# Nine instead of eight up tiles in seven half products, in a new order, and another step into the MLP

## The chip, the cores and the metric

The kernel runs on one core of a Trainium2 chip. PE (TensorE) multiplies; DVE (VectorE), ACT (ScalarE) and POOL (GpSimd) work element by element; SP only issues DMA transfers, and POOL issues some too. The metric is the device time of one execution in microseconds; where several runs are shown, their median.

## The reference

One layer of an encoder trunk over 512 tokens of width 1024, in float32: an RMS norm, one input projection, three groups of attention heads, an output projection into the residual; then the part that the change touches, the gated MLP with a causal convolution of width 3, followed by a gated per-layer input.

```python
def conv_gated_mlp(h, w_up, conv_w, conv_b, w_down):
    u = h @ w_up
    S = u.shape[1]
    up = jnp.pad(u, ((0, 0), (CONV_WIDTH - 1, 0), (0, 0)))
    c = conv_b
    for j in range(CONV_WIDTH):
        c = c + conv_w[j] * up[:, j:j + S]
    gate, val = jnp.split(c, 2, axis=-1)
    return (jax.nn.silu(gate) * val) @ w_down
...
        h = h + conv_gated_mlp(rms_norm(h, ln_ffn[i]), w_up[i], conv_w[i], conv_b[i], w_down[i])
        gate = jax.nn.sigmoid(rms_norm(h, ln_ple[i]) @ w_ple_gate[i])
        h = h + (p[i] @ w_ple_proj[i]) * gate
```

`w_up` is 1024 x 5632, `w_down` 2816 x 1024.

## The kernel before, in words

Every float32 operand of a product is split into a high part (`hi`, fp32r, a cast on ACT) and a low part (`lo`, the difference, on DVE), and a product is three matmuls: hi x hi, hi x lo and lo x hi. Weights come in by DMA on SP's queue into a ring of 7 raw tiles, and their splits go into a ring of 7 pairs (`NRAW`, `NHI`). So a split waits for a landed load and for a free pair, and a load for a raw tile whose split is done.

The attention stage runs first, in slots. Its PE order is written out; the order on ACT and DVE is the scheduler's. In its slots 20 to 45 SP also copies sums' first terms from DRAM to DRAM (`COPIES`, `copy_sum`), dealt out evenly over what `_sums` lists: four copies for every tile of `SEVEN`, and four for each of four groups of down weights.

The step into the MLP is written out by hand (from `add_sums()` to the last `ple_unit`), and its order on PE, ACT, DVE, POOL and SP is kept. The last output products (`last_out`) and the squares of the residual run; a matmul with ones (`total`) adds the squares over partitions into `pst`; `roots` makes the inverse root (a logarithm and an exponential on ACT, four operations on DVE) into `rb2`; `norm(k)` makes row block k of the normed residual `hn` and casts it to `Th`, `low(k)` gives `Tl`. Meanwhile PE multiplies the per-layer input: `ple_product(j)` makes the eight products `pp` of six matmuls each, `ple_keep(j)` copies one out of PSUM on ACT (`pps`) and stores it by SP; `ple_unit(j)` is both. `first_split(f, i)` splits piece i of the weights of up tile f, for the first two tiles.

The MLP has 22 up tiles of 128 gate and 128 value columns. The first two are done together, row block by row block, as `Th` comes. Each of the others goes one of two ways:

- plain (`up_plain`, letter P, three pieces): gate and value columns, 8 row blocks, three matmuls each, 48 matmuls of 512 tokens; weights of 768 + 768 + 512 columns.
- in seven half products (`up_seven`, letter S, six pieces): gate and value as a 2 x 2 block product over even and odd row blocks and two halves of the tokens, by a scheme of Strassen's kind with 7 products instead of 8. 84 matmuls of 256 tokens; weights of four times 768 and once 512 columns, of which the last 2048 come from `usum`, sums of weight blocks in DRAM. These sums are made by transfers that add (`add_sums`, issued by POOL, two in flight, four for each S tile and eight for each down group) on top of the copies. ACT copies results out of PSUM and DVE adds them (`su`) before the convolution.

Either way a chain follows (`ff_chain`: start on ACT, two taps on DVE for each of gate and value, SiLU, product), and for each pair of tiles the left operands of the down products (`left`). The down products (`Down`, letter D) use the same seven-product scheme, in groups of up tiles 0-5, 6-11, 12-17 and 18-21.

`ORDER` gives the order of these pieces on PE: it is kept as written. `tiles_of(ORDER)` numbers the tiles 2 to 21 as their first pieces come, so the letters also say which tiles are S. Everything else in the MLP (loads, splits, copies, chains, additions) is set in order by the planner at the end of the kernel: it gives each task a due time from the PE order and its list of estimated costs, then takes at each step, among tasks that could start about now, the one due first. The engines then keep that order.

Of the kernel before, what the change touches and what calls it, by code (L numbers as in the profile page):

```python
# [45 lines left out]
PHASES = (0, 6, 12, 18, 22)  # L46


ORDER = ("PPPPSSSSSPPSPPSSSSPSPPSPPDDDDDDDSPSSSSDSDDDPDDDSSSSSPSPPSSSSSPSPSSSDSSDDDSDPDDDDDDDDDPPPSSSSSPPSPSSSPSSPSPPPPPPP")


def tiles_of(order):

    f, n, tiles = 2, {"P": 0, "S": 0}, {"P": [], "S": []}
    for c in order:
        if c in n:
            if n[c] == 0:
                tiles[c].append(f)
                f += 1
            n[c] = (n[c] + 1) % {"P": 3, "S": 6}[c]  # L60
    assert f == NF and not any(n.values()), (f, n)
    return tiles["P"], tiles["S"]


PLAIN, SEVEN = tiles_of(ORDER)

# [11 lines left out]
def kernel(ctx: ExitStack, tc: tile.TileContext, x, xt0, xt, pt_in, small, bias_c,  # L78
# [35 lines left out]
    def bank(tag, name):  # L114
        return ps.tile([P, 512], F32, tag=tag, bufs={"z": 2, "s": 2, "t": 3, "o": 1}[tag], name=name)
# [122 lines left out]
    def mm3(acc, ah, al, bh, bl, first, last, **k):  # L238
        pe.matmul(acc, ah, bh, start=first, stop=False, **k)
        pe.matmul(acc, ah, bl, start=False, stop=False, **k)  # L240
        pe.matmul(acc, al, bh, start=False, stop=last, **k)
# [675 lines left out]
    def mtmp(dt, m, name):  # L917
        return mp.tile([P, S * m], dt, tag="conv", bufs=CONV, name=name)
# [8 lines left out]
    def total(tag, sums):  # L927

        pst = bank(tag, "pst")
        pe.matmul(pst, onec.broadcast_to([P, P]), sums, start=True, stop=True)  # L930
        return pst

    def roots(pst, rb, mt, sq):

        act.activation(rb, pst, AF.Ln, scale=1.0 / D, bias=epsc)
        dve.tensor_scalar(mt, pst, 1.0 / D, EPS, ALU.mult, ALU.add)
        act.activation(rb, rb, AF.Exp, scale=-0.5)
        dve.tensor_tensor(out=sq, in0=rb, in1=rb, op=ALU.mult)
        dve.scalar_tensor_tensor(sq, sq, -0.5, mt, ALU.mult, ALU.mult)
        dve.scalar_tensor_tensor(rb, sq, 1.5, rb, ALU.add, ALU.mult)  # L940
# [20 lines left out]
    def ple_product(j):  # L961
        PP[j] = acc = bank("tttzsttt"[j], f"pp_{j}")
        for k in range(2):
            a, b = (w[:, j % 4 * P : (j % 4 + 1) * P] for w in WPP[j // 4, k])
            mm3(acc, a, b, *pT[k], k == 0, k == 1)

    def ple_keep(j):
        pp = mtmp(F32, 1, f"pps_{j}")
        act.copy(pp, PP[j])
        sp.dma_start(out=pp_d[j], in_=pp)  # L970

    def ple_unit(j):
        ple_product(j)
        ple_keep(j)
# [279 lines left out]
    def up_plain(f):  # L1254

        ws, w, more = plain_weights(f)
        us = Slot("z"), Slot("s")

        def some(g, ks):
            def do():  # L1260
                c = g * NF + f
                if ks[0] == 0:
                    U[c] = bank("zs"[g], f"u{c}")
                for k in ks:
                    mm3(U[c], *w(g, k), Th[k // 4][:, k % 4, :], Tl[k // 4][:, k % 4, :], k == 0, k == KD - 1)
            return do

        for g in range(2):
            pe_task(36, some(g, range(6)), [more()], (), [us[g]])
            yield  # L1270
        last = []
        more()
        for g in range(2):
            last.append([pe_task(12, some(g, range(6, KD)), [ws[2]], (), (), [us[g]])])
        ff_chain(f, None, last, ((us[0],), (us[1],)))
        yield
# [131 lines left out]
    def first_split(f, i, later=False):  # L1408
        w = first_w[f][0][i]
        lows = [] if later else None  # L1410
        w.hi, w.lo = split(w.t, w.n, lows=lows)
        w.split.end = 0.0
        return lows[0] if later else None

    def two_adds():
        for q in [q for q in EARLY_ADDS if q.end is None][:2]:
            q.do()
            q.end = 0.0
# [22 lines left out]
        last_sq = sq  # L1441
    todo[7]()
    two_adds()
    for j in range(3):
        ple_unit(j)
    first_split(1, 0)
    ple_unit(3)
    rb2, work = (mp.tile([P, 7, H], F32, tag=tag, bufs=3, name=f"rb2_{tag}").rearrange("p j c -> p (j c)") for tag in ("ah", "al"))
    rb2 = rb2[:, :S]
    roots(total("o", sums), rb2, work[:, :S], work[:, S : 2 * S])  # L1450
    ple_unit(4)
    last_low = first_split(1, 1, True)
    norm(0)
# [91 lines left out]
    def down_pieces():  # L1545
        for ph in range(2):
            for n in range(2):
                d = Down((ph,), n, DT)
                for what in PRODUCTS:
                    d.product(what)  # L1550
                    yield

        for n, whats in enumerate(FIRST):
            DL.append(Down((2, 3), n, ({"X": "z", "Y": "s", "Z": "o"} if n else DT)))
            for what in whats:
                DL[n].product(what, (2,), False)
                yield

    DL = []
    pieces = {"P": (f for f in PLAIN for _ in up_plain(f)), "S": (f for f in SEVEN for _ in up_seven(f)), "D": down_pieces()}  # L1560
    for c in ORDER:
        next(pieces[c])
# [263 lines left out]
```

## Time and profile before

| | us |
|---|---|
| three runs | 695.25, 696.63, 696.77 (median 696.63) |
| profiled execution | 695.37 |
| its span | 693.6 |
| PE, DVE, ACT, POOL busy | 679.1, 560.6, 410.9, 236.0 |
| attention stage ends, about | 297 |
| first up product | 309.47 |
| last down product ends | 644.3 |

Times in the profile count from the span's start. Names are those of the program with buffer numbers left out; nearly all instructions have line 104, that of the helper that records them, so tiles and times tell them apart: `u` are plain up products, `sX`, `sY` and `sZ` those in seven halves, `dn_X`, `dn_Y`, `dn_Z` down products, `pp` the per-layer input's products, `pg` the gate's at the end. `w_hi` and `w_lo` are the splits of weights. A row of a timeline is start, length, engine, line, operation, output<-inputs, shapes and count, with the idle time before it and what ended that in brackets. A row of the chain is start, length and what.

### The profile page before, as it was taken

Reading aid. Unit: us, or ns where it says so; the run is one execution under the profiler, and the core shown is the slowest. Engines: PE = TensorE matmul, PEld = TensorE weight load, DVE = VectorE, ACT = ScalarE, POOL = GpSimd, SP = SyncE. Lnnn points to the kernel's source line nnn. Section 1 sums busy time; section 2 is a strip of 40 time slices with the busy share of each in tenths; the row PEclk is TensorE's granted clock in tenths of the full one; section 3 lists DMA queues with packets and bytes.
Section 4 is the critical chain, followed back from the end, with each engine's and each line's share of the span. In section 5 each row is a group of like instructions: output and inputs, shape, how many; then the busy total and the mean of one; then the engine's idle time right before and its main releaser. Section 6 shows DMA issues by size and latency. Waiting matters only on the chain.

```text
span 693.6 us, 12203 instructions
## 1 busy us (share of the span) xinstructions
PE 679.1 (98%) x4244; PEld 618.3 (89%) x4244; DVE 560.6 (81%) x1168; ACT 410.9 (59%) x799; POOL 236.0 (34%) x349
## 2 busy tenths in 40 slices
PE   8999999999999999999999999999999999999997
PEld 8988988988999988878899899989998898999886
DVE  6679887888878875689788987898888889888873
ACT  6656766767656754475476655456554566556821
POOL 5586675767575540231212111221112200000210
PEclk9999999999999999999999999999999999999999
DMA  9553579746745184279999799997999874462431
GB/s 307 216 168 98 155 241 265 232 165 162 287 136 178 44 266 138 91 184 242 175 269 244 133 266 241 274 232 176 248 278 277 181 197 140 141 234 99 156 122 60
DMA packets 57112, 133.84 MB, mean 193 GB/s; under 512 B 6454, under 2 KB 8118, under 8 KB 57052
## 3 DMA queue, kind: packets, MB, share of 16 engines
q1 hardware_dynamic: 45660, 107.60, 47.0%
q0 software_dynamic: 11104, 25.17, 22.2%
q8 instruction: 33, 0.54, 0.3%
q10 hardware_dynamic: 288, 0.30, 0.1%
q14 instruction: 27, 0.22, 0.1%
HBM read 125.83 MB, written 44.05 MB: 245 GB/s over the span
## 4 chain that ended last, share of the span: by engine, by line
PE 83%; DVE 8%; ACT 3%; POOL 3%; issue 2%; DMA 1%; SPq 0%; DVEq 0%; POOLq 0%; ACTq 0%
PE u L104 22%; PE dn_X L104 9%; PE pg L104 6%; PE C_z L104 5%; PE wo L104 5%; PE sX L104 5%; PE dn_Y L104 4%; PE B_z L104 4%; PE sY L104 3%; PE sZ L104 3%; PE A_z L104 3%; PE dn_Z L104 2%; PE A1b_z L104 1%; PE C_s L104 1%; PE B_s L104 1%
## 5 line engine op out<-in xcount | busy, mean ns | idle before, releaser
L104 DVE TENSOR_TENSOR w_lo<-w_raw,w_hi 128x768 fp32r<-128x768 f32 (+5 forms) x154 | 115.0, 786 | 9.5 <-ACT w_hi L104 9.3
L104 ACT CAST w_hi<-w_raw 128x768 fp32r<-128x768 f32 (+5 forms) x154 | 99.8, 687 | 35.9 <-PE sX L104 6.7
L104 PE MATMUL u<-Th,w_hi 128*128 128x512 f32 x224 | 87.0, 391 | 0.4 <-ACT Th L104 0.4
L104 PE MATMUL u<-Tl,w_hi 128*128 128x512 f32 x224 | 86.9, 390 | 0.0
L104 PE MATMUL u<-Th,w_lo 128*128 128x512 f32 x224 | 86.8, 390 | 0.0
L104 PEld LDWEIGHTS u<-Th,w_hi 128*128 128x128 f32 x224 | 42.0, 188 | 9.1 <-ACT Th L104 0.9
L104 PEld LDWEIGHTS u<-Th,w_lo 128*128 128x128 f32 x224 | 42.0, 188 | 9.0
L104 PEld LDWEIGHTS u<-Tl,w_hi 128*128 128x128 f32 x224 | 42.1, 188 | 8.1
L104 DVE SCALAR_TENSOR_TENSOR c<-u,cols,c 128x511 f32<-128x511 f32 (+1 forms) x56 | 41.0, 746 | 6.2 <-ACT c L104 5.7
L104 POOL DMA_DIRECT2D usum<-usum x16 | 13.0, 812 | 92.5 <-DMA usum<-in_w_up_dram 56.7
L104 PE MATMUL dn_X<-g_ah,w_hi 128*128 128x256 f32 x144 | 39.8, 276 | 0.0
L104 PE MATMUL dn_X<-g_ah,w_lo 128*128 128x256 f32 x144 | 39.8, 276 | 0.0
L104 PE MATMUL dn_X<-g_al,w_hi 128*128 128x256 f32 x144 | 39.8, 276 | 0.0
L104 PE MATMUL B_z<-B_h,Th 128*128 128x384 f32 x96 | 34.4, 358 | 0.8 <-DVE B_zn L104 0.6
L104 PE MATMUL C_z<-C_h,Th 128*128 128x384 f32 x96 | 34.3, 357 | 0.0
L104 POOL TENSOR_TENSOR sums<-sums,n_sq 128x512 f32<-128x512 f32 x3 | 3.9, 1291 | 86.9 <-ACT n_sq L104 86.8
L104 PE MATMUL B_z<-B_h,Tl 128*128 128x384 f32 x96 | 32.3, 337 | 0.0
L104 PE MATMUL C_z<-C_h,Tl 128*128 128x384 f32 x96 | 32.3, 337 | 0.0
L104 PE MATMUL C_z<-C_l,Th 128*128 128x384 f32 x96 | 32.2, 336 | 0.0
L104 PE MATMUL B_z<-B_l,Th 128*128 128x384 f32 x96 | 32.2, 335 | 0.0
L104 ACT ACTIVATE c<-u,cols 128x512 f32<-128x512 f32 x28 | 21.5, 775 | 16.0 <-PE u L104 14.6
L104 POOL DMA_DIRECT2D dsum<-dsum x16 | 13.0, 813 | 47.2 <-DMA dsum<-dsum 20.0
(504 smaller groups left out, 2384.0 us busy)
## 6 DMA issues: line engine op xcount, KB each, us to landing
w_raw<-in_w_up_dram SPq DMA_DIRECT2D x44, 384.0 KB, 6.1
dsum<-in_w_dsum_dram SPq DMA_DIRECT2D x12, 768.0 KB, 7.9
w_raw<-dsum SPq DMA_DIRECT2D x24, 384.0 KB, 5.0
usum<-in_w_usum_dram SPq DMA_DIRECT2D x32, 256.0 KB, 6.1
w_raw<-in_w_down_dram SPq DMA_DIRECT2D x18, 384.0 KB, 4.9
w_raw<-usum SPq DMA_DIRECT2D x16, 384.0 KB, 7.7
B_r<-in_w_in_dram SPq DMA_DIRECT2D x12, 384.0 KB, 3.6
C_r<-in_w_in_dram SPq DMA_DIRECT2D x12, 384.0 KB, 6.1
```

Of the source, the lines that this page charges most:

```text
L104: ins = getattr(self.eng, op)(*a, **k)
```

## The change

`ORDER` is another string. It has 33 letters P instead of 36 and 54 S instead of 48, so eleven plain tiles and nine in seven products; tile 15 changes its way, and all others keep theirs. The pieces stand in another order in several places; after the down products of the second group (eleven in a row now, nine before) come tiles 15 and 16, both S, with no plain piece until the last product of tile 16. `_sums` gets four copies and four adding transfers for tile 15, ahead of those of tile 16, and the copies are dealt out anew over slots 20 to 45: the first twelve stay, the rest shift. The number of weight loads, splits, copies from PSUM and additions follows the tiles.

In the step into the MLP, the split of tile 1's first piece is issued after two gate-input units instead of three; the fourth product's copy out of PSUM and its store come after `roots` instead of ahead of `total`. PE's order there stays as it is.

```diff
-ORDER = ("PPPPSSSSSPPSPPSSSSPSPPSPPDDDDDDDSPSSSSDSDDDPDDDSSSSSPSPPSSSSSPSPSSSDSSDDDSDPDDDDDDDDDPPPSSSSSPPSPSSSPSSPSPPPPPPP")
+ORDER = ("PPPPSSSSSPPSPPPSSSPSSPSPPDDDDDDDPSSSSSDPDSDDDDDSSSSSPSPSSSSPSPSPSSSSSDDDPSDDDDDDDDDDDSSSSSSSSSSSPSPPSSSSSPSPPPPPPPP")
...
     todo[7]()
     two_adds()
-    for j in range(3):
+    for j in range(2):
         ple_unit(j)
     first_split(1, 0)
-    ple_unit(3)
+    ple_unit(2)
+    ple_product(3)
     rb2, work = (mp.tile([P, 7, H], F32, tag=tag, bufs=3, name=f"rb2_{tag}").rearrange("p j c -> p (j c)") for tag in ("ah", "al"))
     rb2 = rb2[:, :S]
     roots(total("o", sums), rb2, work[:, :S], work[:, S : 2 * S])
+    ple_keep(3)
     ple_unit(4)
     last_low = first_split(1, 1, True)
     norm(0)
```

## The prediction

> **What bounds the kernel now.** I read the page's busy times first, then busy time by stretch, then the chain that ended last, and at last the timelines of single engines around the two places that are edited. In the stretch rows the columns are the stretch, its length, then busy time and instructions of PE, weight load, DVE, ACT and POOL, the granted clock, the DMA share and GB/s.
>
> ```profile
> PE 679.1 (98%) x4244; PEld 618.3 (89%) x4244; DVE 560.6 (81%) x1168; ACT 410.9 (59%) x799; POOL 236.0 (34%) x349
> 68.40:297.09 228.69, 224.31 (x1311) 204.60 (x1310) 176.63 (x517) 144.61 (x342) 129.26 (x189) 1.00 0.59 181
> 309.47:644.30 334.83, 334.83 (x2269) 308.00 (x2270) 288.82 (x459) 193.93 (x322) 51.90 (x63) 1.00 0.84 212
> 496.11:558.42 62.31, 62.31 (x442) 57.98 (x441) 53.69 (x87) 33.86 (x58) 13.04 (x16) 1.00 0.99 246
> ```
>
> From 309.47, the first up product, to 644.30, the last down product, PE is busy for all of 334.83 us at full clock. In that stretch a matmul taken away is time taken away, as long as no wait appears. DVE is next with 288.82 us, 86%. Between 496 and 558 us DVE has 53.69 of 62.31 and the DMA share is 0.99. Before the MLP PE has idle time: 228.69 - 224.31 = 4.38 us between 68.4 and 297.09.
>
> **The change: the up tile.** Tile 15 goes from plain to seven half products. The chain's rows (start, length, what) show the plain tile 15 whole, and the seven products of tile 16:
>
> ```profile
> 522.86 10.91 PE u L104 x48
> 533.77 1.39 PE sX L104 x12
> 535.17 2.72 PE sZ L104 x24
> 537.89 1.36 PE sY L104 x12
> 539.25 1.36 PE sX L104 x12
> 540.61 1.36 PE sY L104 x12
> 550.16 1.40 PE sX L104 x12
> 506.54 4.08 PE dn_X L104 x36
> 572.16 24.51 PE u L104 x108
> ```
>
> Plain: 48 matmuls of 512 columns at 24.51/108 = 0.227 us, 10.89 us. Seven products: 84 of 256 columns at 4.08/36 = 0.1133 us, 9.52 us. Gain 1.37 us. The rows also show about 0.03 us (1.39 against 1.36) where 512- and 256-column work alternate; the old order has 36 such borders, the new one 34, so 0.06 us more. Sum of the order: -1.43 us.
>
> [...] The half matmul costs just half of the whole one: 0.1133 against 0.227, no fixed part per instruction. [...]
>
> What the seven-product form needs beside PE: five weight tiles instead of three, so two more ACT casts and DVE subtractions of 768 columns, four ACT copies from PSUM, two 256-column and one 512-column DVE additions.
>
> ```profile
> L104 DVE TENSOR_TENSOR w_lo<-w_raw,w_hi 128x768 fp32r<-128x768 f32 x81 | 75.9, 953 | 8.2 <-ACT w_hi L104 8.1
> L104 DVE TENSOR_TENSOR su<-sX,su 128x256 f32<-128x256 f32 x16 | 6.8, 423 | 3.4 <-ACT su L104 3.2
> L104 DVE TENSOR_TENSOR su<-sX,su 128x512 f32<-128x512 f32 x8 | 5.5, 691 | 5.7 <-PE sX L104 5.7
> L104 ACT CAST w_hi<-w_raw 128x768 fp32r<-128x768 f32 x80 | 65.4, 833 | 25.6 <-PE dn_X L104 5.5 <-PE dn_Y L104 4.3 <-PE u L104 3.5
> 554.56 3.50 DVE L104 TENSOR_TENSOR w_lo<-w_raw,w_hi 128x128 fp32r<-128x128 f32 x7
> 559.78 4.11 PE u L104 x18
> 500.32 2.49 DVE L104 TENSOR_TENSOR w_lo<-w_raw,w_hi 128x512 fp32r<-128x512 f32 x4
> 501.72 2.75 PE u L104 x12
> 515.34 0.95 DVE L104 TENSOR_TENSOR w_lo<-w_raw,w_hi 128x768 fp32r<-128x768 f32 x1
> ```
>
> DVE: 2 x 0.953 + 2 x 0.423 + 0.691 = 3.44 us more; ACT: 2 x 0.833 us and four short copies, on an engine that is busy for 58% of the MLP. Over the MLP DVE goes to 292.3 of 333.4 us, 88%: I cost it at nothing, covered by 41 us of idle DVE. Where the cover is thin: tiles 18 and 19, whose splits end at 554.56 + 3.50 = 558.06 and whose first plain product starts at 559.78, 1.7 us later. Even 0.7 us has been enough: the split of tile 13's last piece is the first of the four at 500.32, ends at 501.0 by the 0.69 us of a 512-column subtraction, and its product follows at 501.72 without a wait. Tile 15's first split ended at 516.3, 6.5 us ahead of 522.86, so the two sevens that now follow the eleven down products in a row begin with a good lead.
>
> **Transfers.** The new tile needs four more copies of 256 KB from DRAM to DRAM in the attention stage (slots 26 to 45 are dealt out anew), four more adding transfers in the MLP, and 768 KB more of loads.
>
> ```profile
> L838 SPq DMA_DIRECT2D usum<-in_w_usum_dram x32: 490/586/1351, 68.4 to 218.1; - x32
> SPq L838 <- DMA usum<-in_w_usum_dram: 1.7, 3, 0.8
> POOL usum L104 <- DMA usum<-in_w_up_dram: 56.7, 9, 8.7
> 488.38 0.81 POOL L104 DMA_DIRECT2D usum<-usum  x1 [4.60 <-DMA usum<-usum]
> 554.54 0.81 POOL L104 DMA_DIRECT2D dsum<-dsum  x1 [0.47 <-DMA dsum<-dsum]
> 530.07 3.01 SPq L104 DMA_DIRECT2D w_raw<-usum  x3
> 576.20 4.83 SPq L104 DMA_DIRECT2D w_raw<-dsum  x4
> ```
>
> The copies cost SP 4 x 0.586 = 2.3 us of issue; what else is queued on SP there are weight and bias loads. I take nothing for it, as a DMA-bound PE wait does not show there, and bound it by the 4.38 us of PE idle time in that stage, gained or lost again. The adding transfers queue on POOL, two in flight, behind nothing but each other, one every 3.9 us (17 from 488.38 to 554.54): those of tiles 16 and 18 and of the last two down groups come some 16 us later. Tile 18's were issued by 488.38 and are loaded at 530.07; the last group's, issued by 554.54, are wanted in the loads after 576.20. Both hold 16 us. Nothing. The ninth sign change of a column triple on POOL near 7 us lies ahead of a POOL wait.
>
> **The step into the MLP.** The split of the second first tile moves ahead of the third gate-input copy, and the fourth copy behind the two root activations. The timelines of ACT, DVE and PE:
>
> ```profile
> 301.78 1.55 ACT L104 COPY pps<-pp 128x512 f32<-128x512 f32 x3
> 303.21 0.85 ACT L104 CAST w_hi<-w_raw 128x768 fp32r<-128x768 f32 x1
> 303.94 0.61 ACT L104 COPY pps<-pp 128x512 f32<-128x512 f32 x1
> 304.42 0.72 ACT L104 ACTIVATE rb_ah<-pst,epsc 128x512 f32<-128x512 f32 x1
> 304.10 0.96 DVE L104 TENSOR_TENSOR w_lo<-w_raw,w_hi 128x768 fp32r<-128x768 f32 x1 [1.23 <-ACT w_hi L104]
> 305.17 0.69 DVE L104 TENSOR_SCALAR rb_al<-pst 128x512 f32<-128x512 f32 x1
> 308.01 0.75 DVE L104 SCALAR_TENSOR_TENSOR hn<-h,cols,rb_ah 128x512 f32<-128x512 f32 x1
> 308.80 0.62 ACT L104 CAST Th<-hn 128x512 fp32r<-128x512 f32 x1 [1.79 <-DVE hn L104]
> 302.53 1.02 PE L104 MATMUL pst<-sums,onec 128*128 128x512 f32 x2
> 308.64 0.39 PE L104 MATMUL pp<-pT_ah,w_lo 128*128 128x512 f32 x1
> 309.47 1.21 PE L104 MATMUL u<-Th,w_hi 128*128 128x512 f32 x4 [0.44 <-ACT Th L104]
> ```
>
> The sum `pst` is there at 302.53 + 1.02 = 303.55, but the logarithm starts at 304.42, right behind the fourth copy, which holds ACT from 303.94: 0.48 us. Without it the logarithm starts at 303.94. DVE would be in its way if its subtraction stayed at 304.10; the cast it waits for moves up by one copy (0.48 us, three in 1.55), to 302.73, so DVE too is free 0.48 us earlier. All that follows, roots, `hn`, the cast of `Th`, moves by 0.48, and the first up product goes from 309.47 to 308.99. PE can take that: its last `pp` matmul starts at 308.64 and the next could at 308.87. The fourth copy now stands behind the second activation, at about 305.2; it frees a bank of which the first up product has need at 308.99, 3 us later, and its store on SP waits 1.3 us longer, in a queue whose next entries wait for four later copies anyway. The third copy, 0.7 us later, frees a bank for the last `pp` product, six matmuls ahead of 308.87, at 307.5. Both covered. -0.48 us; the gap itself, 0.60, bounds the gain, and 0 the other end.
>
> **The sum.** -1.43 - 0.48 = -1.91 us against the profiled execution's 695.37 us, which gives 693.46. It lies 1.26 us below the median of 696.63, so by the median 694.7 us, -0.27%. A change of under 0.2% (1.39 us: 695.24 to 698.02) can't be told from none here.
>
> **Rivals.**
> 1. *DVE falls short from tile 15 to tile 19* (slower side). Two sevens in a row have 3.44 us more DVE work, and PE comes 1.4 us sooner: 4.8 us. If the planner can use none of DVE's 8.6 idle us in that stretch, a cover of 1.7 us leaves a stall of 3.1 at tile 19 (697.8), a cover of 0.7 us one of 4.1 (698.8). It decides from 3.3 us on. For it: covers of 0.7 to 1.7; against: that idle time, and a lead of 6.5. Chance 0.12 over 3.3 us, 0.12 for a smaller stall (695.3 to 698).
> 2. *Transfers bind the run of down products and sevens.* 768 KB of loads and four adds of 256 KB at 246 GB/s are 3.2 + 4.3 = 7.5 us of transfer time where the share is already 0.99; less the lead of 6.5 us, a stall of 1.0: 695.7. Against: after 560 the adds are done. Chance 0.07. [...]
> 3. *The attention stage comes out in another order.* Its ACT and DVE orders are the scheduler's, and copies moved on SP shift landings. PE idle there from nothing to twice 4.38 us: 690.3 to 699.1. Chance 0.10 slower than 698, 0.07 about as before.
> 4. *The step brings nothing*, another chain is 0.5 us behind: 695.2, in the forecast's range.
>
> Forecast with case 4: 0.52, own range 693.6 to 695.2. Faster 0.52; same 0.12 + 0.07 + 0.07 = 0.26; slower 0.12 + 0.10 = 0.22. From 693.2 (some of the attention stage's idle time gained) to 698.8, inside the price of rivals 1 and 3, about 2 in 10 are left out.
>
> **What would show it.** Right: first up product some 0.5 us sooner after `pst`, the logarithm directly behind `pst`; PE busy for all of the MLP, now near 333.4 us; seven products of 1.36 us for tile 15. Wrong: a wait of PE on a split or on ACT between tiles 15 and 19 (rival 1), ACT casts that wait for landings there (rival 2), or a first up product shifted by more than 0.5 us through waits before 297 us (rival 3).

## The result and the profile after

The changed kernel takes 702.54 us (median of five runs, 699.76 to 704.83), against 696.57 for the kernel before on the same chip: ratio 1.0077 (1.0054 to 1.0100). It is slower by 0.5 to 1.0%; forecast was 694.7 us, and the range ended at 698.8.

The profiled execution is the fastest of the five, 699.76 us, 4.39 above that of before. The stages divide this: attention stage +1.43 (the first `pp` starts at 298.52, before at 297.09), the step into the MLP -0.48 (11.91 us from there to the first up product, before 12.38), the MLP 337.99 us instead of 334.67, and about 0.1 behind it. First the page's row of engines and the stretch from the first up product to the first `pg` of the kernel after, then the same stretch of before (columns as in the prediction):

```profile
PE 679.5 (97%) x4280; PEld 619.3 (89%) x4280; DVE 565.1 (81%) x1172; ACT 412.5 (59%) x804; POOL 241.9 (35%) x354
310.43:648.42 337.99, 334.98 (x2305) 308.95 (x2305) 292.69 (x463) 195.29 (x327) 55.02 (x67) 1.00 0.87 216
```
```profile
309.47:644.14 334.67, 334.67 (x2269) 307.83 (x2269) 288.82 (x459) 193.76 (x322) 51.74 (x63) 1.00 0.84 212
```

PE, which never waited here before, now has 3.0 us without work. Each wait costs a little more than it lasts, since the first two matmuls behind it start 0.22 instead of 0.11 us apart. From start to start of all matmuls, against 0.1133 us per 256 columns, the waits make 4.5 us: 0.46 at tile 14, 1.46 at tile 15, 0.26 at tile 16, 2.28 ahead of the last group of down products. The matmuls of the stage, counted at 0.1133 us per 256 columns, make 333.19 us before and 331.83 after. Steps of under 0.08 us between them add 1.36 us before and 1.59 after.

The waits of PE in the MLP (total, times, longest), and tile 15 in the chain of work:

```profile
PE sX L104 <- DVE su L104: 1.2, 1, 1.2
PE dn_X L104 <- DVE w_lo L104: 1.0, 1, 1.0
PE dn_X L104 <- ACT w_hi L104: 0.8, 1, 0.8
```
```profile
524.35 1.36 PE sX L104 x12
525.71 2.72 PE sZ L104 x24
528.43 1.37 PE sY L104 x12
...
530.74 0.73 ACT w_hi L104
...
532.37 0.95 DVE w_lo L104
533.32 0.34 DVE su L104
533.66 0.04 issue
533.71 3.09 PE sX L104 x24
```

The products cost what was forecast (1.36 us each). But the product at 533.71, the seventh, adds into the PSUM bank `sX`. It may not start before DVE has read that bank, and DVE adds its content to the copy (`su`) that ACT makes of the sixth product. The sixth is through at 532.35, and PE stands for 1.2 us. On DVE a subtraction that runs until 533.32 stands ahead of the addition. In e5_dve and e13_costs, where DVE is free when the copy is done, the delay is 1.2 instead of 1.46 us, so about 1.2 are the dependence and 0.26 the order on DVE. In the old order each tile in halves has a plain or down piece between its fifth and sixth piece; in the new one the pieces of tile 15 stand side by side.

The last group. ACT's rows first (start, length, operation, idle time before it), then DVE's, then PE's:

```profile
589.53 0.82 ACT L104 CAST w_hi<-w_raw 128x768 fp32r<-128x768 f32 x1
597.33 0.78 ACT L104 ACTIVATE c<-u,cols 128x512 f32<-128x512 f32 x1 [6.98 <-PE u L104]
599.38 1.04 ACT L104 CAST xh<-sm 128x1024 fp32r<-128x1024 f32 x1
593.68 2.05 DVE L104 SCALAR_TENSOR_TENSOR c<-u,cols,c 128x511 f32<-128x511 f32 x3
598.15 3.50 DVE L104 SCALAR_TENSOR_TENSOR c<-u,cols,c 128x511 f32<-128x511 f32 x5 [2.41 <-ACT c L104]
602.43 1.22 DVE L104 TENSOR_TENSOR xl<-sm,xh 128x1024 fp32r<-128x1024 f32 x1
609.67 0.38 PE L104 MATMUL dn_X<-xh,w_hi 128*128 128x256 f32 x1 [0.78 <-ACT w_hi L104]
611.13 0.39 PE L104 MATMUL dn_X<-xh,w_lo 128*128 128x256 f32 x1 [0.96 <-DVE w_lo L104]
```

ACT stands idle for 7 us in front of the start of the last up tile, which PE has not finished. Behind it in ACT's queue is the cast `xh<-sm` of tiles 18 and 19, whose input was complete at 593.8. DVE stands 2.4 us behind ACT, then works almost without a pause (0.18 us) until the last group's operands are split, some 2 us late. In the kernel before the same cast and subtraction are done well ahead:

```profile
589.15 1.05 ACT L104 CAST xh<-sm 128x1024 fp32r<-128x1024 f32 x1 [1.83 <-DVE sm L104]
592.52 1.22 DVE L104 TENSOR_TENSOR xl<-sm,xh 128x1024 fp32r<-128x1024 f32 x1
```

The step did as forecast. The logarithm now starts 0.40 us behind the end of `pst` (303.96 + 1.02 = 304.98), it was 0.87. It still stands right behind a copy on ACT, now the third one (304.91), as in the forecast, which had it 0.39 us behind `pst`; from the start of `pst` to the first up product it is 310.43 - 303.96 = 6.47 us instead of 309.47 - 302.53 = 6.94:

```profile
303.96 1.02 PE L104 MATMUL pst<-sums,onec 128*128 128x512 f32 x2
304.91 0.60 ACT L104 COPY pps<-pp 128x512 f32<-128x512 f32 x1
305.38 0.71 ACT L104 ACTIVATE rb_ah<-pst,epsc 128x512 f32<-128x512 f32 x1
310.43 0.73 PE L104 MATMUL u<-Th,w_hi 128*128 128x512 f32 x2
```

The attention stage. The largest new step there is 1.14 us at 146. The chain of the kernel after has the load of `bias_B`, which SP issues behind copies, and the work that hangs on it; POOL waited 1.8 us for it, before 0.6. The rest of the +1.43 is in part the spread of single profiles: ahead of the first copy, at 68 us, PE is 0.69 us earlier than in the kernel before, and by 75 us only 0.12. The chain:

```profile
137.19 7.33 DMA bias_B<-fk_d
...
144.64 0.64 POOL dg L561
145.28 0.68 POOL B_e L104
...
146.04 0.62 POOL B_k_k L104
...
146.71 0.50 PE B_s L104 x2
```

### The profile page after: what moved, and what is told of

Its sections match the earlier page's. It is cut to its first block, busy times and chain, and to the rows that moved or that the text cites. A ratio compares the mean times of both kernels' runs of the same rounds, so it can differ in the third digit from the quotient of the medians.

```text
span 698.0 us, 12317 instructions
## 1 busy us (share of the span) xinstructions
PE 679.5 (97%) x4280; PEld 619.3 (89%) x4280; DVE 565.1 (81%) x1172; ACT 412.5 (59%) x804; POOL 241.9 (35%) x354
## 4 chain that ended last, share of the span: by engine, by line
PE 78%; DVE 8%; POOL 4%; DMA 3%; ACT 3%; issue 3%; SPq 0%; POOLq 0%; DVEq 0%; ACTq 0%
PE u L104 20%; PE dn_X L104 8%; PE pg L104 6%; PE wo L104 6%; PE C_z L104 5%; PE sX L104 5%; PE B_z L104 4%; PE dn_Y L104 4%; PE sZ L104 3%; PE sY L104 3%; PE dn_Z L104 2%; PE pp L104 2%; DMA h<-in_x_dram 1%; PE C_s L104 1%; DMA bias_B<-fk_d 1%
## 5 line engine op out<-in xcount | busy, mean ns | idle before, releaser
L104 DVE TENSOR_TENSOR w_lo<-w_raw,w_hi 128x768 fp32r<-128x768 f32 (+5 forms) x155 | 117.3, 792 | 7.7 <-ACT w_hi L104 7.2
L104 PE MATMUL u<-Th,w_hi 128*128 128x512 f32 x208 | 80.8, 391 | 0.0
L104 PE MATMUL u<-Tl,w_hi 128*128 128x512 f32 x208 | 80.6, 390 | 0.0
L104 PE MATMUL u<-Th,w_lo 128*128 128x512 f32 x208 | 80.6, 390 | 0.0
L104 PEld LDWEIGHTS u<-Th,w_lo 128*128 128x128 f32 x208 | 39.1, 188 | 8.3
L104 PEld LDWEIGHTS u<-Th,w_hi 128*128 128x128 f32 x208 | 38.9, 188 | 8.0 <-ACT Th L104 0.4
L104 PEld LDWEIGHTS u<-Tl,w_hi 128*128 128x128 f32 x208 | 39.1, 188 | 7.5
L104 DVE SCALAR_TENSOR_TENSOR c<-u,cols,c 128x511 f32<-128x511 f32 (+1 forms) x52 | 38.0, 745 | 8.7 <-ACT c L104 8.1
L104 POOL DMA_DIRECT2D usum<-in_w_up_dram x18 | 15.2, 861 | 42.7 <-DMA dsum<-dsum 16.6
L104 POOL DMA_DIRECT2D dsum<-in_w_dadd_dram x16 | 14.0, 874 | 43.6 <-DMA usum<-usum 11.1
```

Source lines behind the costliest of these rows:

```text
L104: ins = getattr(self.eng, op)(*a, **k)
```

## The experiments

All times are medians; each ratio is to the kernel before on the same chip, with its interval. In the table the columns tile 14 to last group are PE's delays in us, worked out from the starts of all matmuls in the trace as above; "other" gives place and size; "half clock" is a stretch of 3.41 us in the MLP at half the granted clock right behind a wait, which costs some 1.7 us more (last section). The MLP stage is from the first up product to the first `pg`. The kernel before took 695.73 to 696.57 us on the five chips.

| kernel | tile 14 | 15 | 16 | last group | other | MLP | time | ratio |
|---|---|---|---|---|---|---|---|---|
| before | 0 | 0 | 0 | 0 | | 334.67 | 696.57 | |
| after | 0.46 | 1.46 | 0.26 | 2.28 | | 337.99 | 702.54 | 1.0077 (1.0054-1.0100) |
| e1_step | 0 | 0 | 0 | 0 | | 334.68 | 695.60 | 0.9997 (0.9981-1.0012) |
| e2_order | 0.47 | 1.47 | 0.52 | 2.29 | | 338.03 | 701.42 | 1.0078 (1.0053-1.0102) |
| e3_copies | 0.46 | 1.47 | 0.50 | 2.28 | at 410, 521: 1.72 | 339.72 | 700.47 | 1.0063 (1.0043-1.0083) |
| e4_cover | 0.46 | 0 | 2.29 | 2.29 | | 338.64 | 701.59 | 1.0093 (1.0059-1.0127) |
| e5_dve | 0.46 | 1.20 | 0 | 2.28 | | 337.61 | 699.81 | 1.0061 (1.0038-1.0084) |
| e6_form | 0 | 0 | 1.66 | 2.9, half clock | | 339.46 | 699.99 | 1.0054 (1.0034-1.0074) |
| e7_eight | 0.47 | 0 | 0 | 2.3, half clock | | 340.73 | 700.08 | 1.0051 (1.0033-1.0069) |
| e8_free | 0 | 0 | 0 | 0 | | 334.64 | 695.18 | 0.9983 (0.9970-0.9996) |
| e9_left | 0.46 | 1.47 | 0.52 | 2.45 | at 515: 0.42 | 338.84 | 701.33 | 1.0085 (1.0063-1.0106) |
| e10_eight_left | 0.47 | 0 | 0 | 2.4, half clock | | 339.35 | 701.29 | 1.0078 (1.0059-1.0097) |
| e11_late | 0 | 0 | 0 | 0.60 | | 335.26 | 696.90 | 1.0012 (0.9999-1.0025) |
| e12_both | 0 | 0 | 1.66 | 2.45 | | 338.83 | 698.70 | 1.0037 (1.0023-1.0051) |
| e13_costs | 0 | 1.19 | 0 | 0 | 352: 0.9; 447: 2.9; 521: 0.3 | 338.61 | 702.33 | 1.0097 (1.0083-1.0112) |
| e14_before_costs | 0 | 0 | 0 | 0 | 354: 1.3 | 336.69 | 699.75 | 1.0051 (1.0034-1.0068) |
| e15_all | 0 | 0 | 0 | 0 | 352: 1.1 | 335.32 | 696.07 | 1.0012 (0.9998-1.0027) |
| e16_after_all | 0 | 0 | 0 | 0 | 354: 0.9; 523: 3.1, half clock | 338.96 | 700.20 | 1.0065 (1.0041-1.0088) |
| e17_late_costs | 0 | 0 | 0 | 0 | | 333.99 | 695.42 | 0.9986 (0.9972-1.0000) |
| e18_eight_costs | 0 | 0 | 0 | 0 | | 335.72 | 697.46 | 1.0023 (1.0010-1.0036) |

The delays do not make up all of the MLP column. The small steps between matmuls (1.36 us in the kernel before, 1.3 to 1.7 in most) add up to 2.0 to 3.1 us in e7, e12, e14, e15, e17 and e18; in these, many matmuls of the last 35 us of the stage start 4 to 6 ns late. Why is open.

**The parts one by one.** e1_step is the kernel before with the step's edit, e2_order with the new `ORDER` alone.

> The kernel before with the step into the MLP of the change alone. If the step does what was forecast (the logarithm directly behind the sum's product, the first up product 0.45 us sooner, the same distance kept to the end): 696.1 us, 0.4 to 0.5 below the kernel before. If another chain right behind it takes the gain back: 696.6. If the step itself has a part in the loss: above 697.

> The kernel before with the new order of pieces alone, the old step. If the loss is all the order's and the step gains 0.45 us: about 703 us, 6 above the kernel before. If step and order only lose together (the step shifts the MLP against its transfers): near 697.

The MLP's loss is all in the order: 338.03 us with it alone, 334.68 with the step alone. The step shortens its own stage by 0.47 us in every kernel that has it (11.91 us from the first `pp` to the first up product, 12.38 without), which is within the uncertainty of the whole time.

e3_copies is the changed kernel with the copies of the other tiles back in their old slots and those of tile 15 in slots 39, 42, 44 and 45. e4_cover puts the first piece of tile 16, two products, between tile 15's fifth and sixth piece (the expectations of e6 and later runs call this same edit one product of tile 16):

```diff
+        i = SEVEN.index(15)
...
+        for q in (0, 0, 0, 0, 0, 1, 0):
+            yield next(units[i + q])
```

> The changed kernel with tile 15's four copies in late slots (39, 42, 44, 45) and all others dealt out as before. If the 1.4 us that the attention stage lost come from the shifted copies on SP (the bias load issued at 137.19 instead of 136.16): the first up product some 1.4 us sooner, near 309.0, and 701.2 us. If the scheduler's order there is the cause, or tile 15's copies at any place: no change, 702.5.

> The changed kernel with the first piece of tile 16 (two products, 2.7 us of PE) between the fifth and the sixth piece of tile 15, which stand side by side in the new order. If PE's wait of 1.35 us there is the dependence of the last product on the copy and addition of the one just before, with nothing between: that wait goes, and 701.1 us. If DVE is short of time there in any case: the wait comes back some products later, and no change.

With the copies in their old slots POOL's wait for the bias load fell from 1.8 to 0.9 us and the stage ended 1.0 us sooner than in the changed kernel (first `pp` at 297.50), but the MLP got a new wait of 1.4 us on a landing at 521. So copies ahead of the bias load do delay it; that they are the whole of the 1.43 us is not shown, for the first `pp` starts between 295.8 and 297.9 us in other kernels that have the old copies and no stretch at half clock there. Over all profiles POOL's wait was 1.4 to 2.8 us (mean 1.9) in the six with shifted copies, 0.5 to 1.6 (1.0) in the nine with the other tiles' copies in their old slots, and 0.3 to 0.8 (0.5) in the five with slots 26 to 29 free.

e4_cover settles tile 15 in part: the wait on the sum of the product just before goes, and 2.29 us come back at tile 16, some 7 us later. PE waits there for tile 16's bank `sY`, which ACT has to copy out. That copy stands in ACT's queue behind a start of tile 15's chain, for which ACT was idle for 4.59 us until DVE's sum was there. So the cover only moved the wait to the next place.

**Has DVE too much to do?** Two sevens in a row have 3.44 us more DVE work. e5_dve takes 4.5 us off DVE at tile 15, e6_form keeps the old order with tile 15 in halves, e7_eight keeps the new order with tile 15 plain; e8_free is the kernel before with the step and no copies in slots 26 to 29.

```diff
e5_dve
+                if zero:
+                    act.activation(lo, t[:, i * P : j * P], AF.Copy, scale=0.0)
e6_form, ORDER behind the second group's down products
-DDDDDDDDDPPPSSSSSPPSPSSSPSSPSPPPPPPP
+DDDDDDDDDSSSSSSSSSSSPPSPSSSPSSPSPPPPPPP
e7_eight
-DDDDDDDDDDDSSSSSSSSSSSPSPPSSSSSPSPPPPPPPP
+DDDDDDDDDDDPPPSSSSSPSPPSSSSSPSPPPPPPPP
e8_free
+FREE_SLOTS = [q for q in range(*COPY_SLOTS) if not 26 <= q < 30]
```

> The changed kernel, but the five low parts of tile 15's weights are set to zero by ACT instead of being subtracted by DVE, so that DVE loses 4 x 0.953 + 0.69 = 4.5 us of work between about 500 and 525 us and ACT gains some 4 us; the matmuls stay. The output leaves out the low parts of tile 15's weights. Theory (the ninth tile in halves gives DVE more than it can do from tile 15 on, and the backlog of the 3.4 us reaches the end of the MLP): the stall of 0.94 + 1.12 us ahead of the last group's first products goes, those at tiles 15 and 16 shrink, and the time falls by 2 to 4 us against the changed kernel, to about 697 to 699. Rival (the new order itself has places where a product needs the sum of the one just before it, and DVE's load has nothing to do with it): the stalls stay, 1.35 us at tile 15 and 2.07 us at the last group, and the time stays within 1 us of the changed kernel's.

> The kernel before with one part of the change alone: tile 15 in seven half products in its old place, the rest of the old order, the old step, and all other copies in their old slots; one product of tile 16 stands between the fifth and the sixth piece of tile 15, so that no product needs the sum of the one just before it. Theory (the ninth tile overloads DVE wherever the pieces stand): stalls of 2 us or more after tile 15 and at the last group, MLP stage of 335 us or more, time 696.5 to 698.5 against 695.7 before. Rival (the new order is at fault, not the ninth tile): no stalls, an MLP stage of 333.4 us, time about 694.3.

> The changed kernel with tile 15 plain again, three pieces at the place of its six: eight tiles in halves in the new order, copies dealt out as before, the new step. Theory (the ninth tile overloads DVE): no stalls from tile 15 on and none at the last group, MLP stage about 335 us, time about 695.5 to 696.5. Rival (the new order is at fault): stalls of 2 us or more remain, at the last group above all, MLP stage of 337 us, time 697.5 to 699. The bias load in the attention stage should come as in the kernel before in both cases, 8.4 to 8.8 us after the first of the three weight loads ahead of it, since the copies are dealt out as there; in the changed kernel it was 9.8.

> The kernel before with the new step, and with no copies in slots 26 to 29, the slots just ahead of the bias load at 136 us; the 48 copies are dealt out over the other 22 slots. Theory (copies on SP's queue ahead of the bias load delay it, and PE waits for what is made from it): the bias load comes 3 us or more earlier against the weight loads around it, the wait of POOL on it (0.63 us before) goes, the attention stage ends up to 0.6 us sooner, and with the step's 0.5 us the time is 0.5 to 1.1 us below the kernel before. Rival (the load has slack in the kernel before, so that only the changed kernel's later copies cost something): attention stage as in the kernel with the step alone, time 0 to 0.5 us below before; more copies in the other slots could also delay other loads there, up to 1 us slower.

Neither of the two theories stood. With 4.5 us less on DVE the wait at tile 16 goes, 1.20 us stay at tile 15, and the last group waits for 2.28 us as before: DVE simply idles more (busy for 292.0 instead of 295.5 us from 309 to 650). With eight tiles in halves the last group waits as long (e7), and with the old order and nine tiles it waits even longer (e6). So what is late at the last group is neither the ninth tile's work as such nor the new order as such; both only set it off. e8_free is the best of the simple kernels: 0.17% less than before (ratio 0.9970 to 0.9996), with the step's 0.47 us in it. POOL's wait for the bias load was 0.3 us, but its profile ends the attention stage at 297.06 us, before at 297.09: POOL waits 2.7 us for a later load (`bias_C`, at 184 us) instead, and PE 1.2 us for POOL. So a gain by the freed slots is not shown.

**One cast moved.** e9_left and e10_eight_left make the left operands of tiles 18 and 19 due 8 us sooner in the changed kernel and in e7_eight; e11_late makes them due 2 us later in the kernel before; e12_both is e6_form with that, the step and e8_free's copies.

```diff
+        if f == 18:
+            SHIFT.extend((a, b, c))
...
+    for q in SHIFT:
+        q.dl += -8.0
```

> The changed kernel with one due time moved: the left operands of tiles 18 and 19 are due 8 us sooner, so that on ACT the cast of tile 18's sums stands ahead of the last up tile's two starts instead of behind them, and on DVE the subtraction that follows stands two taps into that tile instead of five. Theory (the wait ahead of the last group's first products is made by this order: ACT stands 7 us idle for PE with a cast behind it whose input is there, and DVE does 1.2 us of it late): the two waits of 0.94 + 1.12 us become 0.3 to 1.1 us in sum, the MLP stage 336.9 to 337.5 us against 338.1, time some 1 us under the changed kernel's, or more where a wait had been followed by a stretch at half clock. Rival (DVE simply has too much to do by then): the waits stay at 2 us.

> The changed kernel with tile 15 plain again (as in the run with eight) and the left operands of tiles 18 and 19 due 8 us sooner. Theory (the order on ACT and DVE behind tile 18): the waits of 1.00 + 1.12 us ahead of the last group shrink to 1.1 us or less in sum, no stretch at half clock follows, and the MLP stage goes from 340.6 us to 336 to 337 us. Rival (the order of the pieces on PE itself): waits as in the run with eight.

> The kernel before with the left operands of tiles 18 and 19 due 2 us later and nothing else: PE's order, the number of instructions and the copies are untouched; on ACT the cast of tile 18's sums now stands behind the last up tile's starts, as in the changed kernel. Theory: a wait of 0.5 to 2 us ahead of the last group's first products appears in a kernel that has none, the MLP stage is 335.3 to 337 us against 334.8, time 696.5 to 698.5. Rival (the order there is covered, the ninth tile's or the new order's DVE work is what is late): no wait, time within 0.3 us of the kernel before.

> Tile 15 in seven half products in the old order (one product of tile 16 ahead of its last piece), the new step, no copies in slots 26 to 29, the new tile's own copies in slots 39 to 45, and the left operands of tiles 18 and 19 due 8 us sooner. Theory: the wait of 1.55 us at tile 16 stays, the 2.4 us at the last group shrink to 1.2 or less and no stretch at half clock follows, so that the MLP stage is 335 to 336.3 us, up to 1.5 us longer than before, which the step (0.5) and the copies (0.4) make up: 695 to 696.5 us, no better than the kernel before with the step and the moved copies (695.2). If the ninth tile were worth the 1.43 us that PE saves: 694 us.

My theory that this one cast was the cause fell: the cast moved ahead, and the wait stayed at 2.45 us. The rows of ACT and DVE of e9_left show why:

```profile
595.43 1.05 ACT L104 CAST xh<-sm 128x1024 fp32r<-128x1024 f32 x1 [3.45 <-DVE sm L104]
595.31 0.74 DVE L104 SCALAR_TENSOR_TENSOR c<-u,cols,c 128x511 f32<-128x511 f32 x1
596.51 1.23 DVE L104 TENSOR_TENSOR xl<-sm,xh 128x1024 fp32r<-128x1024 f32 x1 [0.45 <-ACT xh L104]
599.77 4.80 DVE L104 SCALAR_TENSOR_TENSOR c<-u,cols,c 128x511 f32<-128x511 f32 x7 [2.04 <-ACT c L104]
```

DVE again stands 2 us for ACT's start of the last tile, and now three taps of the tile before, whose inputs are there, are queued behind it (seven in the group instead of the last tile's four). In e10_eight_left and e12_both the delay at the last group stayed at 2.4 us too. e11_late shows the same from the other side: the kernel before, with not an instruction added and only this order changed, waits 0.60 us; its time can't be told from that of the kernel before.

**The planner's estimates.** In all these kernels the planner had put ready work behind work that waits for PE. Its estimate for a DVE operation is 0.16 us + 1.04 ns a column, 0.96 us for 768, and for a cast on ACT 0.84. That is near what one operation lasts. But the next one starts sooner: two subtractions in 1.83 us are 1.83 - 0.95 = 0.88 us apart, two casts 1.56 - 0.82 = 0.74 us (rows of the kernel after):

```profile
531.49 1.83 DVE L104 TENSOR_TENSOR w_lo<-w_raw,w_hi 128x768 fp32r<-128x768 f32 x2
530.63 1.56 ACT L104 CAST w_hi<-w_raw 128x768 fp32r<-128x768 f32 x2
```

So the planner reckons DVE and ACT slower by a tenth than they are. By my reading of its code it then believes them behind PE where work is dense: the last tile's starts seem ready with everything else, and due times alone decide. No run records what the planner believed; the runs show only what its orders do. e13 and e14 give the planner the measured spacings (in the changed kernel, and in the one before), e15_all is e12_both without the moved due times, e16_after_all is the changed kernel with e3's copies and e4's cover, both with the measured spacings too.

```diff
-        return "dve", 0.16 + n * 0.00104
+        return "dve", 0.07 + n * 0.00104
-        return "act", 0.2 + n * 0.00083
+        return "act", 0.1 + n * 0.00083
-        TAP = ("dve", 0.76)
+        TAP = ("dve", 0.66)
```

> The changed kernel with the planner's estimates set to what the traces show from one instruction's start to the next: DVE 0.07 instead of 0.16 us + 1.04 ns a column, ACT 0.10 instead of 0.20 us + 0.83 ns a column, a tap 0.66 instead of 0.76, a start 0.68 instead of 0.78, SiLU 0.53 instead of 0.63. PE's order, the instructions and the copies are the same; only the orders on ACT, DVE and the queues may differ. Theory (the too high costs make the planner put ready work behind work that waits for PE): the waits of 2.06 us at the last group and those at tiles 14 and 16 go, that of 1.35 us at tile 15 stays (each of its last two products needs the sum of the one before), MLP stage 334.5 to 335.5 us against 338.1, time 698 to 699.5 with the copies' delay in the attention stage. Rival (DVE really has too much to do): waits of 2 us or more stay, time within 1 us of 702.

> The kernel before with the same measured costs in the planner and nothing else. It has no waits of PE in the MLP that the planner could take away, so both theories expect the time of the kernel before within 0.2%, 695 to 697.5 us, MLP stage 334.8 us; it is the control that the costs alone bring nothing by another way. A better order at its end could take 0.3 us.

> Tile 15 in seven half products in the old order, one product of tile 16 ahead of its last piece, the new step, no copies in slots 26 to 29, the new tile's copies in slots 39 to 45, and the measured costs in the planner. Theory: no wait of PE on DVE or ACT in the MLP is left, MLP stage 333.4 us, 1.4 less than before; with the step's 0.5 and some 0.4 from the copies 693.5 to 694.8 us, faster than both kernels. Rival (DVE really has too much to do with nine tiles in halves): waits of 1.5 us at tile 16 and 2 us at the last group stay, 697 to 699 us as in the last run of this kind.

> The changed kernel with the measured costs in the planner, one product of tile 16 ahead of tile 15's last piece, and tile 15's copies in slots 39 to 45 with the others where they were before. Theory: the waits at tile 15, at tile 16 and at the last group go together, MLP stage 333.4 to 334 us, time 694 to 695.5, which is what the change was forecast to give. Rival (DVE has too much to do): 699 us or more.

The waits at tiles 14 and 16 and at the last group are gone in all of them, with nine tiles in halves and in both orders; in e13_costs the 1.19 us at tile 15 stay, which is the dependence. So these waits come from the order that the planner writes with its costs, and not from too much work. My times were wrong nevertheless, and none of the four is faster than the kernel before: other waits come where there were none (that the measured costs leave no margin is my explanation, not shown), 0.9 to 1.3 us at tiles 4 and 5 in all four (also in the kernel before, so the control came out over 2 us above its forecast, with a stretch at half clock in the attention stage besides), and 2.9 and 3.1 us on a late landing. The chain of e16_after_all:

```profile
511.51 12.41 DMA w_raw<-usum
...
524.03 0.84 ACT w_hi L107
...
525.76 0.69 DVE h L107
526.46 0.14 issue
526.59 3.57 PE dn_X L107 x16
```

A load of sums took 12.4 us to land; ACT's cast, DVE's subtraction and, queued behind that on DVE, the addition that frees PE's bank all waited for it.

e17_late_costs and e18_eight_costs keep the old costs up to tile 9 and use the measured ones from tile 10, once on e15's kernel with nine tiles in halves, once on e8_free's with eight.

> The run with everything mended (nine tiles in halves in the old order, one product of tile 16 ahead of tile 15's last piece, the new step, no copies in slots 26 to 29), with the planner's old costs up to tile 9 and the measured ones (DVE 0.09 and ACT 0.10 us less an instruction) from tile 10 on. Theory (the ninth tile is worth the 1.43 us of PE time once nothing waits): no waits at tiles 4 and 5 as in the kernel before, none later, MLP stage 333.4 us, time 693.8 to 695.0, some 1.2 us under the same kernel with eight tiles. Rival (something else, landings above all, takes it back): a wait of 1 us or more behind tile 10, time 695.5 or more.

> The kernel before with the new step, no copies in slots 26 to 29, and the measured costs in the planner from tile 10 on: the same as the other run with eight tiles in halves instead of nine. Both theories: MLP stage 334.8 us as in the kernel before, time 694.8 to 695.7. It is the kernel that the other run is to be compared with.

The MLP's stretch of e17_late_costs and of e18_eight_costs:

```profile
311.74:645.73 333.99, 333.99 (x2305) 309.07 (x2305) 294.44 (x465) 198.23 (x329) 58.58 (x71) 1.00 0.86 219
```
```profile
308.52:644.24 335.72, 335.72 (x2270) 308.98 (x2270) 291.60 (x461) 195.07 (x324) 55.34 (x67) 1.00 0.84 212
```

With nine tiles in halves PE doesn't wait once, DVE has 294.4 us of work in 334.0, and the pair differ by 1.7 us in this stage and 2.0 in time. So in this pair the ninth tile brings what PE saves. What stays open: e18's stage is 1.05 us longer than that of before without any wait over 0.08 us but the one of 0.11 us at the start, in steps of 4 to 6 ns a matmul, and its time was 1.8 us above my forecast. So the worth of the ninth tile is better taken from e17 against the kernel before: 0.68 us in the stage, where the matmuls save 1.36 and the small steps take 0.68 of it (2.04 us, before 1.36), and 0.14% in time, with an interval that reaches 1.0000. Against e8_free, its counterpart with the planner's old costs, it brings nothing that can be seen (695.42 against 695.18, ratios 0.9986 and 0.9983).

## Why the prediction was wrong

- *PE's saving* (-1.43): right as a term. The products of tile 15 took 1.36 us each, and at the measured 0.1133 us the count of matmuls gives 333.19 and 331.83 us, -1.36. The part of 0.06 for two borders fewer is not there; the steps at borders add up to 0.1 us in both kernels. The saving was then lost three times over in waits, 4.5 us; that PE would be busy for all of the MLP was the condition on which the term stood.
- *DVE's 3.44 us, "costed at nothing, covered by 41 us of idle DVE"*: this is the step that failed. The size was near: DVE's busy time in the stage went from 288.82 to 292.69 us. The cover was not there. DVE and ACT take their work in the order that the planner wrote, so idle time counts only where the next instruction in that order could run (ahead of the last group ACT idled for 3.5 us with a ready cast queued). The cover should have been read per queue: what stands behind an instruction that waits for PE. DVE has enough time (e17), but the order that the planner gave it doesn't use it; 2.28 us at the last group, some 0.7 at tiles 14 and 16. I had looked at tiles 15 to 19 and taken the list of estimated costs as given, without setting it against the spacing in the trace.
- *The two sevens "begin with a good lead"*: I looked at weights only and missed the dependence inside a tile. With the fifth and the sixth piece side by side, PE waits for ACT and DVE to add the product just finished: 1.46 us, of which 1.2 are the dependence. The letters of the order showed it.
- *Transfers at nothing*: wrong in the attention stage, which lost 1.43 us, within the bound that I had given. Copies ahead of the bias load are behind a step of 1.14 us there; e3 ended the stage 1.0 us sooner, but profiles with old copies differ by 2.1 us among themselves, so the size stays open. In the MLP the adds held in the changed kernel; in two others a landing of 12.4 us came to bind at 521 to 523 us, in the run of down products that the second rival names, at 1.4 us (e3) and 3.1 (e16) instead of 1.0.
- *The step* (-0.48): right, 0.47 us from `pst` to the first up product, by the mechanism that was named: one copy less on ACT ahead of the logarithm.
- *The rivals*: the first had the right engine, but another place and another reason, too much work. Its price (a stall of 3.1 or 4.1 us) came near the 4.5 us of delays by luck, since 1.46 of these are at tile 15, which it didn't count. I gave it 0.12 for the large stall, and the third 0.10; that both came together, and that waits bring half-clock stretches (0.50 over 3.41 us in e7_eight), was outside my range.

## What to carry to other kernels

Where engines take work in a written order, an idle share is no cover (DVE idled for 45 us of the changed kernel's MLP stage, and PE waited 3.0): ask for each queue what stands behind the instruction that waits, and whether the planner that wrote the order has the engine's real spacing from start to start or only the length of one instruction. Before pieces of a product scheme are moved together, list which product needs the sum of which earlier one. And change a dense order together with its cost list, since e13 to e16 show both that orders made with the old costs held these waits and that orders made with other costs held new ones elsewhere.

## What the runs showed of the hardware

In e7_eight two waits of PE of under 1 us each cut its clock from 1.00 to 0.50. Of the granted clock, the profiles of all twenty kernels show the same: counted in stretches of 3.413 us from the moment the clock first became full, each stretch ahead of the last matmul in which PE idles for about half of it or more is followed by one at half clock, which costs about 1.7 us of work (half of its length). That was so for all twelve such stretches (idle 0.497 to 0.85); of all others there, with idle of up to 0.48, none was. Where the kernel ends it is less clear: two stretches that hold the last matmul, with idle of 0.51 and 0.52 (e18 and e9), were not followed by one. The step of 3.413 us is the profiles': in the kernel before the clock is full from 5.40 us and half from 691.48, behind the last matmul, 201 steps later; in e7_eight it is full from 6.10 and half from 610.27, 177 steps later; in e2_order the half clock lasts from 148.18 to 151.59, one step. Two waits of 0.83 and 0.96 us (delays of 1.0 and 1.1) are enough if they fall into one stretch. e7_eight at the last group (1.63 of 3.42 us busy, the next at 0.50), and e13_costs at 145 us, just on the other side (1.78 of 3.41, the next at 1.00):

```profile
606.85:610.27 3.42, 1.63 (x12) 1.23 (x11) 3.31 (x6) 3.19 (x7) 0.00 (x0) 1.00 0.98 354
610.27:613.68 3.41, 3.41 (x19) 3.41 (x18) 2.67 (x5) 2.61 (x4) 0.00 (x0) 0.50 1.04 394
```
```profile
145.26:148.67 3.41, 1.78 (x11) 1.78 (x12) 1.25 (x4) 0.12 (x1) 2.84 (x5) 1.00 0.63 234
148.67:152.08 3.41, 2.87 (x19) 2.43 (x18) 3.28 (x21) 2.54 (x8) 1.06 (x3) 1.00 0.00 1
```

No single gap in these twelve was as long as the stretch (the longest was 2.9 us, in e16); the idle share of the stretch decided. That a kernel whose waits come near this share varies from run to run is my inference. Seven of the twelve stretches lie between 41 and 47 us, ahead of the first copy, and the other thirteen profiles have none there. The changed kernel's profile has no such stretch (its mean clock is 1.000), the other four runs of it have mean clocks of 0.996 to 0.998 and take 2.3 to 5.1 us longer. That these stretches are all of that difference is likely but not shown, as only one run has a trace.
